# A diffusion trunk on one core: conditioning blocks taken later, stores delayed, a shorter lead of filling work in the output projection, and a final norm by products with ones

## The chip, the cores and the metric

The kernel runs on one core of one Trainium2 chip. The metric is the device time of one execution in microseconds (us), the median of several. Engines are named as the profile names them: PE (TensorE matmul) with PEld (its weight loads), DVE (VectorE), ACT (ScalarE), POOL (GpSimd), SP (SyncE, which here only issues DMAs). PEclk is the granted TensorE clock, 1.00 for 2.4 GHz and 0.50 for 1.2 GHz.

## The reference

A trunk of two layers over 1,152 positions (1,024 of a sample and 128 of a prompt), model width 1,024, everything in fp32. Layer 0 has an input projection that feeds attention heads and retention heads, layer 1 a gated MLP; each layer ends its first half with an output projection and its second half is a SwiGLU. Six vectors for each layer (shift, scale and gate, twice) come from the conditioning vector `c` by one product with `w_ada`.

```python
for l in range(DEPTH):
    sh1, sc1, g1, sh2, sc2, g2 = ada_mod(c, w_ada[l], b_ada[l])   # silu(c) @ w_ada + b_ada, 6 x 1024
    h = modulate(rmsnorm(x, norm_g[l, 0]), sh1, sc1)
    y = ab_latent(h, ...) if l % 2 == 0 else chunk_gmlp(h, ...)   # each ends in a product with w_o_ab / w_out_c
    x = x + g1 * y
    h = modulate(rmsnorm(x, norm_g[l, 1]), sh2, sc2)
    x = x + g2 * (silu(h @ w_ffn_gate) * (h @ w_ffn_up)) @ w_ffn_down
y = rmsnorm(x, final_norm_g)                                      # x / sqrt(mean(x*x) + eps) * g
```
The prompt runs through the same code with its own conditioning vector `c_ctx`.

## The kernel before

**Precision and tiling.** Every large product is made of three: an operand is split into a high part, which ACT rounds (CAST), and the low part that remains, which DVE subtracts (TENSOR_TENSOR). A weight tile is called `w0` to `w4` (a ring of five; two halves, high and low), its raw form lands in one of three slots of the tile `ST`. PE can start a weight's group when the high half is there, and goes on when the low half is. A group of products on PE is six matmuls of 288, 384 or 512 columns. Activations are feature-major, 128 features on the partitions; a piece `(c, h)` is 288 positions, c = 0, 1 and h = 0, 1. `x0` to `x3` hold the residual stream, `hq0` to `hq3` and `h0` to `h2` operands of products.

**Order.** The program is written by a planner. `Clocks` keeps a modelled time for each engine (`clk.t["T"]` is PE's); each instruction that is recorded moves it (so nearly all have the helper's line L129). `Stream.pump` goes through the list of weight loads: it issues the next load on SP as soon as one of the three slots is free, and when the load is ready by the model it writes the work on it. An entry of kind "w" is a weight (cast and difference). An entry of kind "pair" is a block of `w_ada`: two loads of 512 KB, and four matmuls in which `S32` (the conditioning vector, 32 columns) meets 512 columns of `ST`. SP issues in program order, so a load whose slot is not yet free keeps everything behind it waiting. `fill` writes work from three queues (squares, norms, splits of activations into high and low parts) as long as the modelled clocks of the other engines stay within `ahead[0]` of PE's (7.0 us; the SwiGLU sets its own). `tick`, after every group of products, calls both.

**Stages.** Up to 240 us: loads, norm, the attention heads' input projection; to 400 us: the other blocks of the input projection (with the second half of layer 0's conditioning), retention; to 735 us: attention; to 855 us: `proj_out` of layer 0; to 1655 us: SwiGLU by seven products of halves in the place of eight; to 1900 us: gated MLP (with layer 1's conditioning); to 2040 us: `proj_out` of layer 1; to 2818 us: the second SwiGLU; then the final norm and the stores.

**The output projection.** For each group of 288 columns, `resid` adds the gated product to `x` (DVE, SCALAR_TENSOR_TENSOR with `mod`), `squares` sums the squares over features for the next norm, and `pspill` stores the piece of `x` to DRAM (`xtd`, SP). When c = 0 is complete, `rscale` norms it and `rsplit` makes the 14 operands of the SwiGLU (sums, differences, high and low parts) as filling work, while PE goes on with c = 1. Four groups use one weight.

**The tail.** In the last projection, `last1` squares each finished piece: ACT makes the square in one of two buffers, multiplies x by the norm's gain, and DVE adds the square to the sum, one piece after the other. `done1` then norms c: `rstd` sums over the partitions by products with ones (96x2), root, reciprocal (both 96x12), a diagonal form, a second product that spreads the result over 128 partitions, and eight multiplications (128x576) whose results are stored on SP.

Of the kernel before, what the change touches and what calls it, by code (L numbers as in the profile page):

```python
# [13 lines left out]
P = 128  # L14
# [118 lines left out]
def body(nc, tc, ap):  # L133
# [88 lines left out]
    class Stream:  # L222
# [11 lines left out]
        def pump(self, force=False):  # L234
            moved = True
            while moved:
# [18 lines left out]
                if self.pi < self.di and self.pi not in self.stops:  # L255
# [4 lines left out]
                    if it["kind"] == "pair":  # L260
                        if self.pi + 1 >= self.di:
                            continue
                        two = self.items[self.pi + 1]
                        if not force and clk.ready([it["v"], two["v"]]) > clk.t["T"]:
                            continue
# [79 lines left out]
    def bg_add(gen):  # L345
        bg.append(gen)
        return gen
# [30 lines left out]

    def tick():
        W.pump()  # L380
        fill()
# [83 lines left out]
    def acc2(c):  # L465
        return SC[:, 1152 * c:1152 * c + 576]

    def piece(c, h):
        return 576 * h + HN * c
# [5 lines left out]
    def xp(f, c, h):  # L475
        return xh(c, f // 4)[:, f % 4, h]

    def xp2(i, c, h):
        return xh(c, i // 2)[:, 2 * (i % 2):2 * (i % 2) + 2, h]

    def pspill(i, c, h):
        o = piece(c, h)
        SY.dma_start(out=xtd[:, 2 * i:2 * i + 2, o:o + HN], in_=xp2(i, c, h))

# [76 lines left out]
    def xnorm(l, w, c):  # L561

        yield from rstd(c)
        A, B = acol[l][w], mod[l][:, 24 * w:24 * w + 8]
# [51 lines left out]
    def rscale(l, c, h):  # L616

        yield from rstd(c, (h,))
        A, B = acol[l][1], mod[l][:, 24:32]
# [1176 lines left out]
    def proj_out(l, bef=None, done=None, ks=range(8), mix=None):  # L1796
# [36 lines left out]
        drain(sq[0])  # L1833
        rplaces(0)
        for z in (FIRST_Q, OTHER_Q):
            bg_add(rsplit(0, z))
# [634 lines left out]


    def last1(c, m):
        for f in (m, m + 4):
            for h in range(2):
                x = xp(f, c, h)
                bg3.append(squares(c, h, f, lambda x=x, f=f: S.activation(x, x, AF.Copy, scale=P2[:, 19 + f:20 + f])))

    def done1(c):
        def gen():  # L2480
            yield from rstd(c)
            for h in range(2):
                r = acc2(c)[:, HN * h:HN * h + HN].unsqueeze(1).to_broadcast([P, 2, HN])
                for i in range(4):
                    x = xp2(i, c, h)
                    V.tensor_tensor(x, x, r, ALU.mult)
                    o = piece(c, h)
                    SY.dma_start(out=ap["o_y"][2 * i:2 * i + 2, :, o:o + HN].rearrange("f p t -> p f t"), in_=x)
                    yield
        g = bg_add(gen())  # L2490
        if c:
            drain(g)

# [58 lines left out]
```

## Time and profile before

| | before |
|---|---|
| median of 3 runs | 2847.53 us (2843.91 to 2848.49) |
| profiled execution | 2844.86 us |
| its span, first to last instruction | 2843.1 us |
| granted clock of PE, mean over the span | 0.983 |
| PE busy | 2689.3 us (95%) |
| DVE, ACT, POOL busy | 1787.7 us (63%), 1167.8 us (41%), 514.5 us (18%) |
| DMA moved | 457.67 MB, mean 161 GB/s |

The profile shows the span in 40 slices, then groups of instructions, the idle time of each engine with what ended it, and the chain of work that ended last. About 2 us of the execution's time lie outside its span. A row of a timeline is one run of like instructions on one engine: start, length, engine, operation, output<-inputs, shape, count, and in brackets the idle time ahead of it with what ended it.

### The profile page before, as it was taken

How to read it: one execution, taken by the hardware profiler on the slowest of the kernel's cores; microseconds unless marked ns; L12 is line 12 of the kernel's file. 1: busy time of each engine (PE TensorE's matmuls, PEld its weight loads, DVE VectorE, ACT ScalarE, POOL GpSimd, SP SyncE). 2: the span in 40 equal slices, each digit the busy share in tenths (PEclk: the TensorE clock that was granted, in tenths of full speed). 3: DMA queues.
4: the chain of work that ended last, by engine and by line, in shares of the span. 5: the costliest groups of instructions: out<-in, count | busy, mean ns of one | idle time of the engine just before them, and what ended most of it. 6: DMA issues, size and time to landing. Idle time of an engine off the chain costs nothing.

```text
span 2843.1 us, 49004 instructions
## 1 busy us (share of the span) xinstructions
PE 2689.3 (95%) x18859; PEld 2536.9 (89%) x18859; DVE 1787.7 (63%) x3606; ACT 1167.8 (41%) x2389; POOL 514.5 (18%) x570
## 2 busy tenths in 40 slices
PE   6989998999999999999999899998999999999996
PEld 5987897988988999999899877798999999999995
DVE  5651235888577565665788763456666666558876
ACT  5552224777455333333322351234544344332224
POOL 1120013665100000000465300000000000016551
PEclk9999998999999999999999999999999999999998
DMA  9386426323433444538877442352334343578761
GB/s 301 90 271 207 131 72 188 90 57 96 156 111 120 144 169 140 181 128 273 270 236 251 142 154 82 111 169 77 113 124 162 108 157 124 189 267 267 233 211 67
DMA packets 455328, 457.67 MB, mean 161 GB/s; under 512 B 25963, under 2 KB 399478, under 8 KB 453558
## 3 DMA queue, kind: packets, MB, share of 16 engines
q1 hardware_dynamic: 400272, 360.83, 41.3%
q10 hardware_dynamic: 54822, 93.70, 8.9%
q8 instruction: 149, 2.44, 0.4%
q14 instruction: 85, 0.70, 0.1%
HBM read 312.52 MB, written 141.93 MB: 160 GB/s over the span
## 4 chain that ended last, share of the span: by engine, by line
PE 62%; DVE 9%; ACT 4%; DMA 4%; issue 2%; POOL 1%; ACTq 0%; SPq 0%; DVEq 0%; POOLq 0%
PE PS L129 62%; DVE x L129 4%; DVE SC L129 2%; DVE w L129 2%; DMA hcd<-SC 2%; ACT x L129 1%; ACT w L129 1%; ACT SC L129 1%; DVE hq L129 1%; POOL ST L129 1%; DMA x<-xtd 0%; DMA w<-krd 0%; DMA ST<-in_w_ada 0%; DVE ST L129 0%; ACTq L129 0%
## 5 line engine op out<-in xcount | busy, mean ns | idle before, releaser
L129 PE MATMUL PS<-hq,w 128*128 128x288 f32 (+1 forms) x10644 | 1547.5, 302 | 62.6 <-ACT SC L129 16.2
L129 PEld LDWEIGHTS PS<-hq,w 128*128 128x128 f32 x10644 | 1484.3, 189 | 99.1 <-ACT w L129 20.8
L129 DVE TENSOR_TENSOR w<-ST,w 128x512 fp32r<-128x512 f32 (+3 forms) x539 | 382.1, 725 | 294.8 <-ACT w L129 290.4
L129 ACT CAST w<-ST 128x512 fp32r<-128x512 f32 (+3 forms) x717 | 375.2, 552 | 420.8 <-POOL ST L129 274.3
L129 DVE SCALAR_TENSOR_TENSOR x<-PS,mod,x 128x288 f32<-128x288 f32 (+2 forms) x944 | 389.5, 445 | 124.5 <-PE PS L129 119.4
L129 POOL TENSOR_TENSOR w<-ST,w 128x256 fp32r<-128x256 f32 (+1 forms) x178 | 126.9, 729 | 1592.2 <-ACT w L129 970.2
L129 PE MATMUL PS<-h,w 128*128 128x288 f32 (+1 forms) x2522 | 386.8, 298 | 10.7 <-DVE SC L129 7.3
L129 PEld LDWEIGHTS PS<-h,w 128*128 128x128 f32 (+1 forms) x2522 | 350.6, 188 | 21.5 <-DVE SC L129 9.7
L129 ACT COPY SC<-PS 128x576 f32<-128x576 f32 (+8 forms) x245 | 124.3, 510 | 259.8 <-PE PS L129 218.5
L129 PE MATMUL PS<-x,w 128*128 128x288 f32 (+1 forms) x1440 | 218.8, 299 | 1.8 <-ACT adac L129 1.4
L129 PEld LDWEIGHTS PS<-x,w 128*128 128x128 f32 x1440 | 203.0, 188 | 4.2 <-ACT h L129 1.8
L129 DVE TENSOR_TENSOR SC<-PS,SC 128x576 f32<-128x576 f32 (+3 forms) x146 | 94.1, 646 | 169.0 <-PE PS L129 149.0
L129 POOL TENSOR_TENSOR ST<-ST 128x256 f32<-128x256 f32 (+1 forms) x192 | 139.9, 729 | 150.6 <-DVE w L129 134.6
L129 PEld LDWEIGHTS PS<-w,hq 128*128 128x128 f32 x648 | 120.5, 188 | 38.9 <-issue 11.4
L129 PE MATMUL PS<-w,hq 128*128 128x512 f32 x648 | 154.6, 396 | 0.0
L129 DVE TENSOR_TENSOR SC<-SC 128x288 f32<-128x288 f32 (+5 forms) x215 | 104.4, 494 | 57.5 <-ACT SC L129 41.4
L129 ACT ACTIVATE SC<-SC 128x576 f32<-128x576 f32 (+2 forms) x89 | 56.9, 639 | 192.2 <-DVE SC L129 180.5
L129 PE MATMUL PS<-w,w 96*128 96x512 f32 x384 | 109.2, 420 | 4.7 <-ACT w L129 2.7
L129 DVE TENSOR_TENSOR SC<-SC,x 128x576 fp32r<-128x576 f32 (+1 forms) x90 | 68.0, 756 | 69.6 <-DMA hcd<-SC 50.7
L129 DVE TENSOR_REDUCE sm<-PS 128x1 f32<-128x1152 f32 (+1 forms) x72 | 89.0, 1236 | 21.9 <-PE PS L129 21.1
L129 ACT ACTIVATE SC<-x 128x288 f32<-128x288 f32 x128 | 55.2, 440 | 114.8 <-DVE x L129 92.4
L129 DVE TENSOR_TENSOR ST<-ST 128x512 f32<-128x512 f32 x144 | 98.8, 686 | 1.8
(191 smaller groups left out, 2475.9 us busy)
## 6 DMA issues: line engine op xcount, KB each, us to landing
hq<-hcd SPq DMA_DIRECT2D x106, 576.0 KB, 9.1
hcd<-x ACTq DMA_DIRECT2D x180, 288.0 KB, 2.2
ST<-in_w_ada SPq DMA_DIRECT2D x80, 512.0 KB, 4.2
h<-hcd SPq DMA_DIRECT2D x48, 576.0 KB, 7.3
ST<-in_w_ffn_gate SPq DMA_DIRECT2D x52, 512.0 KB, 4.0
ST<-in_w_ffn_up SPq DMA_DIRECT2D x52, 512.0 KB, 3.9
hcd<-SC ACTq DMA_DIRECT2D x72, 288.0 KB, 3.3
ST<-in_w_ffn_down SPq DMA_DIRECT2D x80, 256.0 KB, 5.4
```

The lines of the kernel that those rows point to most:

```text
L129: return fn(*args, **kw)
```

## The change

Four things change. A "pair" is written 1.5 us of modelled time later than before. `pspill` no longer stores at once: the stores stand in a list `due`, and `spill_due` issues them from `tick` 3.0 us after they are ready by the model, or at the latest where the norm begins to overwrite the same piece. In `proj_out`, the lead of filling work is 4.5 in the place of 7.0 from the point where c = 0 is complete. The tail is rewritten: of c = 1 only the first half of the squares is summed by DVE; the eight others go to buffers of their own, and ten products with ones (128x288) sum everything over the features and spread it in one step; root and reciprocal are 128x288, once for each h; four multiplications of c = 0 and their stores wait for the tail, and half of the last stores are issued by ACT.

```diff
                         two = self.items[self.pi + 1]
-                        if not force and clk.ready([it["v"], two["v"]]) > clk.t["T"]:
+                        if not force and clk.ready([it["v"], two["v"]]) + 1.5 > clk.t["T"]:
                             continue
...
     def tick():
+        spill_due()
         W.pump()
         fill()
...
+    due = deque()
+
     def pspill(i, c, h):
         o = piece(c, h)
-        SY.dma_start(out=xtd[:, 2 * i:2 * i + 2, o:o + HN], in_=xp2(i, c, h))
+        due.append((c, h, xtd[:, 2 * i:2 * i + 2, o:o + HN], xp2(i, c, h)))
+
+    def spill_due(which=None):
+
+        for z in list(due):
+            if z[:2] == which or which is None and clk.ready([z[3]]) + 3.0 < clk.t["T"]:
+                SY.dma_start(out=z[2], in_=z[3])
+                due.remove(z)
...
     def rscale(l, c, h):
 
+        spill_due((c, h))
         yield from rstd(c, (h,))
...
         rplaces(0)
+        ahead[0] = 4.5
         for z in (FIRST_Q, OTHER_Q):
             bg_add(rsplit(0, z))
...
     def last1(c, m):
+        if c and m > 1:
+            return
         for f in (m, m + 4):
...
     def done1(c):
         def gen():
-            yield from rstd(c)
+            yield from rstd(0)
             for h in range(2):
+                if h:
+                    yield lambda: False
+                yield from scaled_out(0, h, acc2(0)[:, HN * h:HN * h + HN])
+        if c == 0:
+            bg_add(gen())
+            return
+        while bg3:
+            bg_step(bg3)
...
+        late = [(0, 2), (0, 3), (1, 6), (1, 7), (1, 2), (1, 3), (0, 6), (0, 7)]
+
+        def add(h, q, st, sp):
+            TE.matmul(sums[h], lhsT=ones, rhs=q, start=st, stop=sp, skip_group_check=True)
+        for n, (h, f) in enumerate(late):
+            q = SC[:, 1728 + HN * n:][:, :HN] if n < 6 else adac[:, 0:HN] if n == 6 else ST[:, 0, 0:HN]
+            S.activation(q, xp(f, 1, h), AF.Square)
+            add(h, q, n in (0, 2), n in (5, 7))
+            if n == 3:
+                for z in range(2):
+                    add(z, a[:, HN * z:HN * z + HN], False, False)
+        for f in (2, 3, 6, 7):
+            gcol(1, 1, f)
+        for h in (1, 0):
+            S.activation(root[h], sums[h], AF.Sqrt, bias=epsc, scale=1.0 / 1024.0)
+        for f in (2, 3, 6, 7):
+            gcol(1, 0, f)
+        while bg:
+            bg_step()
+        for h in (1, 0):
+            V.reciprocal(root[h], root[h])
+            for _ in scaled_out(1, h, root[h]):
+                pass
```

`scaled_out` holds the four multiplications and stores that stood in `done1`; with c = 1 every other store goes to ACT's queue. `gcol` is the multiplication by the gain.

**Conditioning blocks on PE.** These are PE's rows at the start of the second part of the input projection, 241 us into the run. Rows with `ST_65,S32_92` are a pair; all others are groups of products. Before:

```order
L129 MATMUL PS_74<-hq3_20_535,w4_32_1715 128x384 x6
L129 MATMUL PS_74<-ST_65,S32_92 32x512 x4
L129 MATMUL PS_74<-hq0_13_219,w4_32_1715 128x384 x6
L129 MATMUL PS_74<-hq1_17_331,w4_32_1715 128x384 x6
L129 MATMUL PS_74<-hq2_19_465,w4_32_1715 128x384 x6
L129 MATMUL PS_74<-hq3_20_535,w4_32_1715 128x384 x6
L129 MATMUL PS_74<-ST_65,S32_92 32x512 x4
L129 MATMUL PS_74<-w0_33_1848,hq0_13_219 128x512 x6
L129 MATMUL PS_74<-w3_34_1852,hq1_17_331 128x512 x6
L129 MATMUL PS_74<-w1_35_1856,hq2_19_465 128x512 x6
L129 MATMUL PS_74<-ST_65,S32_92 32x512 x4
```

The same place of the change:

```order
L129 MATMUL PS_74<-hq0_13_219,w4_32_1715 128x384 x6
L129 MATMUL PS_74<-hq1_17_331,w4_32_1715 128x384 x6
L129 MATMUL PS_74<-hq2_19_465,w4_32_1715 128x384 x6
L129 MATMUL PS_74<-hq3_20_535,w4_32_1715 128x384 x6
L129 MATMUL PS_74<-ST_65,S32_92 32x512 x4
L129 MATMUL PS_74<-w0_33_1848,hq0_13_219 128x512 x6
L129 MATMUL PS_74<-w3_34_1852,hq1_17_331 128x512 x6
L129 MATMUL PS_74<-w1_35_1856,hq2_19_465 128x512 x6
L129 MATMUL PS_74<-w2_37_1970,hq3_20_535 128x512 x6
L129 MATMUL PS_74<-ST_65,S32_92 32x512 x4
```

The first pair has moved behind four groups of 384 columns, and the pairs that follow stand four groups of 512 columns apart, where three stood between them.

**Weights in the second output projection on DVE.** These are DVE's rows in `proj_out` of layer 1, 1979 to 1992 us into the run. The rows on `x0` and `x1`, `hq2`, `h0` and `h2` are the filling work of `rsplit`; `w2_142` and `w0_143` are the low halves of the next two weights. Before:

```order
L129 TENSOR_TENSOR x1_102_11573<-x1_102_11573,x0_101_11572 128x2x288 x2
L129 TENSOR_TENSOR hq2_19_465<-x1_102_11573,hq2_19_465 128x2x288 x2
L129 TENSOR_TENSOR h0_138_17472<-x0_101_11572,h0_138_17472 128x576 x2
L129 TENSOR_TENSOR x1_102_11573<-x1_102_11573 128x2x288 x2
L129 TENSOR_TENSOR h2_140_17474<-x1_102_11573,h2_140_17474 128x576 x2
L129 SCALAR_TENSOR_TENSOR x3_104_11716<-PS_74,mod1_94,x3_104_11716 128x288
L129 TENSOR_TENSOR w2_142_17618<-ST_65,w2_142_17618 128x1024
L129 TENSOR_TENSOR SC_66<-SC_66 128x288
L129 SCALAR_TENSOR_TENSOR x3_104_11716<-PS_74,mod1_94,x3_104_11716 128x288
L129 TENSOR_TENSOR w0_143_17650<-ST_65,w0_143_17650 128x1024
```

The same place of the change:

```order
L129 TENSOR_TENSOR x1_102_11573<-x1_102_11573,x0_101_11572 128x2x288 x2
L129 SCALAR_TENSOR_TENSOR x3_104_11716<-PS_74,mod1_94,x3_104_11716 128x288
L129 TENSOR_TENSOR w2_142_17604<-ST_65,w2_142_17604 128x1024
L129 TENSOR_TENSOR hq2_19_465<-x1_102_11573,hq2_19_465 128x2x288
L129 TENSOR_TENSOR SC_66<-SC_66 128x288
L129 TENSOR_TENSOR hq2_19_465<-x1_102_11573,hq2_19_465 128x2x288
L129 TENSOR_TENSOR h0_138_17471<-x0_101_11572,h0_138_17471 128x576 x2
L129 TENSOR_TENSOR x1_102_11573<-x1_102_11573 128x2x288 x2
L129 TENSOR_TENSOR h2_140_17473<-x1_102_11573,h2_140_17473 128x576 x2
L129 SCALAR_TENSOR_TENSOR x3_104_11716<-PS_74,mod1_94,x3_104_11716 128x288
```

The low half of `w2` has moved ahead of eight rows' worth of filling work (`hq2`, `h0`, `x1`, `h2`, two instructions each); that of `w0` stands behind all of it, as before. The low half of `w1`, a little earlier, has moved the other way, behind the norm's sixteen instructions, and `proj_out` of layer 0 shows the like: there the low halves of two weights move forward by some instructions each.

**The tail on DVE.** These are DVE's last rows before the change and in it. `x2` and `x3` are the pieces of c = 1, `x0` and `x1` of c = 0. Before:

```order
L129 SCALAR_TENSOR_TENSOR x3_159_22642<-PS_74,mod1_94,x3_159_22642 128x288 x2
L129 TENSOR_TENSOR SC_66<-SC_66 128x288 x13
L129 RECIPROCAL rs96_100<-rs96_100 96x12
L129 TENSOR_TENSOR SC_66<-ident_87,rs96_100 96x576
L129 TENSOR_TENSOR x2_158_22500<-x2_158_22500,SC_66 128x2x288 x2
L129 TENSOR_TENSOR x3_159_22642<-x3_159_22642,SC_66 128x2x288 x2
```

The same place of the change:

```order
L129 SCALAR_TENSOR_TENSOR x3_159_22642<-PS_74,mod1_94,x3_159_22642 128x288 x2
L129 TENSOR_TENSOR x0_156_22498<-x0_156_22498,SC_66 128x2x288 x2
L129 TENSOR_TENSOR x1_157_22499<-x1_157_22499,SC_66 128x2x288 x2
L129 RECIPROCAL SC_66<-SC_66 128x288
L129 TENSOR_TENSOR x2_158_22500<-x2_158_22500,SC_66 128x2x288 x2
L129 TENSOR_TENSOR x3_159_22642<-x3_159_22642,SC_66 128x2x288 x2
L129 RECIPROCAL SC_66<-SC_66 128x288
```

The thirteen additions behind the last product are gone (five of them stand among the earlier rows, eight are no longer there), two wide reciprocals have come, and each is followed by four multiplications (those after the second are the last four rows).

## Rows read from the trace of the kernel before

**Rows 1.** What PE waited for over the span: the engine and tile that ended the idle time, us in total, times, longest.

```profile
PE PS L129 <- DVE SC L129: 22.6, 13, 10.3
PE PS L129 <- ACT w L129: 22.1, 10, 9.5
PE PS L129 <- DVE w L129: 8.3, 7, 4.1
PE PS L129 <- DMA ST<-in_w_ada: 7.6, 4, 2.9
```

**Rows 2.** PE's timeline from 238 to 267 us (the conditioning blocks of layer 0; rows with ST,S are pairs, whose matmuls leave two records each).

```profile
241.25 2.87 PE L129 MATMUL PS<-ST,S 128*32 128x512 f32 x8 [2.88 <-DMA ST<-in_w_ada]
244.04 5.37 PE L129 MATMUL PS<-hq,w 128*128 128x384 f32 x24
...
254.67 1.05 PE L129 MATMUL PS<-ST,S 128*32 128x512 f32 x4
256.85 1.05 PE L129 MATMUL PS<-ST,S 128*32 128x512 f32 x4 [1.13 <-DMA ST<-in_w_ada]
257.83 4.41 PE L129 MATMUL PS<-w,hq 128*128 128x512 f32 x18
262.17 1.06 PE L129 MATMUL PS<-ST,S 128*32 128x512 f32 x8
```

**Rows 3.** One stretch of a table by windows (us, then the busy time of PE, PEld, DVE, ACT and POOL with counts, the granted clock, the DMA share, GB/s), and the row on loads of `w_ada` from the DMA view of 236 to 290 us (KB each, median us from issue to landing).

```profile
242.60:246.00 3.40, 3.40 (x10) 1.96 (x7) 0.00 (x0) 0.00 (x0) 0.00 (x0) 0.51 0.70 210
...
ST<-in_w_ada SPq DMA_DIRECT2D x16, 512.0 KB, 4.4
```

**Rows 4.** The output projection of layer 0: PE from 797 to 813 us, then DVE in the same stretch.

```profile
803.49 5.65 PE L129 MATMUL PS<-hq,w 128*128 128x288 f32 x22 [4.08 <-DVE w L129]
810.81 2.37 PE L129 MATMUL PS<-hq,w 128*128 128x288 f32 x16 [0.73 <-DVE w L129]
...
797.78 1.42 DVE L129 TENSOR_TENSOR x<-x,x 128x576 f32<-128x576 f32 x2
802.22 1.21 DVE L129 TENSOR_TENSOR w<-ST,w 128x1024 fp32r<-128x1024 f32 x1
806.42 1.42 DVE L129 TENSOR_TENSOR x<-x 128x576 f32<-128x576 f32 x2
```

**Rows 5.** The output projection of layer 1: PE from 1964 to 1998 us, then DVE, then one window (columns as in rows 3).

```profile
1989.33 0.85 PE L129 MATMUL PS<-hq,w 128*128 128x288 f32 x2 [9.47 <-ACT w L129]
1990.73 7.51 PE L129 MATMUL PS<-hq,w 128*128 128x288 f32 x45 [0.56 <-DVE w L129]
...
1983.52 1.43 DVE L129 TENSOR_TENSOR hq<-x,hq 128x576 fp32r<-128x576 f32 x2
1989.46 1.21 DVE L129 TENSOR_TENSOR w<-ST,w 128x1024 fp32r<-128x1024 f32 x1
1991.39 1.21 DVE L129 TENSOR_TENSOR w<-ST,w 128x1024 fp32r<-128x1024 f32 x1
...
1989.30:1993.50 4.20, 3.62 (x13) 3.27 (x14) 4.20 (x8) 2.76 (x5) 0.00 (x0) 0.50 0.35 89
```

**Rows 6.** The conditioning blocks of layer 1, 1836 to 1870 us: PE, then SP's issues.

```profile
1841.70 1.06 PE L129 MATMUL PS<-ST,S 128*32 128x512 f32 x8
...
1856.85 1.75 PE L129 MATMUL PS<-ST,S 128*32 128x512 f32 x8
...
1842.80 0.81 SPq L129 DMA_DIRECT2D ST<-in_w_ada  x2
1848.81 0.38 SPq L129 DMA_DIRECT2D ST<-in_w_in_c  x1
```

**Rows 7.** The tail, 2806 to 2844 us: PE's last four rows, then DVE, ACT and SP.

```profile
2816.88 0.96 PE L129 MATMUL PS<-h,hq 128*128 128x288 f32 x6
2828.10 2.08 PE L129 MATMUL PS<-ones,SC 128*96 128x2 f32 x12 [10.26 <-DVE SC L129]
2831.66 2.29 PE L129 MATMUL PS<-SC,ones 96*128 96x288 f32 x4 [1.47 <-DVE SC L129]
...
2817.68 0.93 DVE L129 SCALAR_TENSOR_TENSOR x<-PS,mod,x 128x288 f32<-128x288 f32 x2
2833.45 5.44 DVE L129 TENSOR_TENSOR x<-x,SC 128x576 f32<-128x576 f32 x8 [1.85 <-ACT SC L129]
...
2819.01 0.44 ACT L129 ACTIVATE SC<-x 128x288 f32<-128x288 f32 x1 [1.97 <-DVE SC L129]
2819.49 0.53 ACT L129 ACTIVATE x<-x,P 128x288 f32<-128x288 f32 x1
...
2834.24 5.09 SPq L129 DMA_DIRECT2D o_y<-x  x8
```

**Rows 8.** DVE's reciprocals, grouped by form over the whole span (output<-input with the shape, count, busy us in all, mean ns of one).

```profile
L129 DVE RECIPROCAL sm<-sm 128x1 f32<-128x1 f32 x72 | 10.5, 156 | 11.4 <-ACT SC L129 11.3
L129 DVE RECIPROCAL rcn<-rcn 128x18 f32<-128x18 f32 x4 | 1.1, 266 | 9.0 <-ACT rcn L129 9.0
```

**Rows 9.** PE, 2801 to 2806 us: one product with ones (96x288, two records) between products at the full clock.

```profile
2802.08 0.65 PE L129 MATMUL PS<-SC,ones 96*128 96x288 f32 x2
2802.35 1.18 PE L129 MATMUL PS<-h,w 128*128 128x288 f32 x6
2803.37 0.65 PE L129 MATMUL PS<-SC,ones 96*128 96x288 f32 x2
```

More of the change, by code (lines that the diff above doesn't have):

```diff
@@ L561, in xnorm @@
     def xnorm(l, w, c):
+        for h in range(2):
+            spill_due((c, h))
         yield from rstd(c)
@@ L616, in rscale @@
     def rscale(l, c, h):
+        spill_due((c, h))
         yield from rstd(c, (h,))
@@ L2470, in body, with gcol, scaled_out @@
     yield "E"
+    def gcol(c, h, f):
+        x = xp(f, c, h)
+        S.activation(x, x, AF.Copy, scale=P2[:, 19 + f:20 + f])
     def last1(c, m):
+        if c and m > 1:
+            return
         for f in (m, m + 4):
             for h in range(2):
-                x = xp(f, c, h)
-                bg3.append(squares(c, h, f, lambda x=x, f=f: S.activation(x, x, AF.Copy, scale=P2[:, 19 + f:20 + f])))
+                bg3.append(squares(c, h, f, lambda h=h, f=f: gcol(c, h, f)))
+    def scaled_out(c, h, r):
+        for i in range(4):
+            x = xp2(i, c, h)
+            V.tensor_tensor(x, x, r.unsqueeze(1).to_broadcast([P, 2, HN]), ALU.mult)
+            o = piece(c, h)
+            (SY if i % 2 or not c else S).dma_start(out=ap["o_y"][2 * i:2 * i + 2, :, o:o + HN].rearrange("f p t -> p f t"), in_=x)
+            yield
@@ L2479, in done1 @@
     def done1(c):
         def gen():
-            yield from rstd(c)
+            yield from rstd(0)
             for h in range(2):
[L2483 to L2489, printed above, removed]
@@ L2490, in done1 @@
-        g = bg_add(gen())
-        if c:
-            drain(g)
+                if h:
[6 more added lines that the diff above has]
+            bg_step(bg3)
+        a = acc2(1)
+        sums = [PS[:, 4 + h, :HN] for h in range(2)]
+        root = [SC[:, 576 + HN * h:][:, :HN] for h in range(2)]
+        late = [(0, 2), (0, 3), (1, 6), (1, 7), (1, 2), (1, 3), (0, 6), (0, 7)]
```

## Prediction

> **What bounds the kernel now.** I read first what PE waits for [rows 1], since PE is busy for 95% of the span: only its idle time and its time at the half clock can be won. Four waits stand out: on sums of squares from DVE, on the high and the low halves of weights, and on conditioning loads. Then I followed each one in the timelines. The conditioning loads stop PE at the start of the second part of the input projection [rows 2]; the halves of weights stop it in both output projections [rows 4, 5]; the sums stop it in the tail [rows 7]. After each of the longer stops the granted clock is 0.50 for some us [rows 3, 5], so a stop costs more than its length.
>
> **The conditioning blocks of layer 0.** PE waits 2.88 us for the first pair, which then takes 2.87 instead of 1.06 us because its second load lands late; of the groups behind it, 3.4 us run at 0.51 of the clock [rows 2, 3]. Four groups of 512 columns would follow at 1.45 us each (257.83 to 262.17 for three), so four of 384 are worth 4 x 1.45 x 384/512 = 4.3 us; they took 5.3 (244.04 to 249.34). The pair at 254.67 ends 3.16 us later, for its second load lands late again. What can be removed: 2.88 + 1.81 + 1.0 + 2.1 = 7.8 us. In the change the first pair stands four groups later, at 241.25 - 2.88 + 4.3 = 242.7; its data were there at 241.25 and, for the second load, some 2 us after. The later pairs stand 4 x 1.45 + 1.0 = 6.8 us apart in the place of 5.3. A pair's loads can start when the one before gives its slots back, and take 0.8 to issue and 4.4 to land [rows 3]: 5.2 us, which just fits into 5.3 and has 1.6 to spare in 6.8. I take -7.5; bounds -8.2 (the casts behind gain a little too) and -4 (the first pair still waits for its second load and brings the half clock with it). What is moved behind them, casts and norm factors, is used tens of us later and hides behind products.
>
> **Layer 1's conditioning blocks** move by a group or more. One of them takes 1.75 in the place of 1.06 us [rows 6], so there is 0.7 to win, twice or three times that if others gain as much, and nothing at worst: -0.7.
>
> **The delayed stores.** On SP they stand in the change behind one or two loads of weights rather than ahead of them. A load can't start before its slot is free, and in the projections that is when the low half of an earlier weight is made; an issue of 0.4 us, like those of weights [rows 6], ahead of it is hidden by that wait. I cost it at nothing; with the cover gone it is eight stores of 0.4 us, 3 us either way. The norm that overwrites a piece now waits for a store that may have been issued late; queued behind it on DVE are the operands of the SwiGLU and the low halves of weights, and PE waits for those. It is the third rival below that would show it.
>
> **The shorter lead, layer 0.** PE stops 4.08 us for the low half of `w1` at 802.22 [rows 4]. In the change it stands ahead of the work at 797.78 and is ready before PE asks at 799.4. The stop then falls on the next weight, `w0`: four groups later PE asks for it at 802.6. DVE has the same work ahead of it as before, but for the work at 806.42 and behind, which it now overtakes: 806.4 + 0.4 + 1.2 = 808.1, where PE went on at 810.81 before. That is 2.5 us earlier; but the stop is now one of 5.5 us and the half clock falls on products that before ran at the full one (22 matmuls took 5.65 us at 803.49, 16 took 2.37 at 810.81). I take -0.5; bounds -2.5 and +1.
>
> **The shorter lead, layer 1.** PE stops 9.47 us for the high half of `w2` and 0.56 for its low half, made at 1989.46 [rows 5]. In the change the low half stands in front of the work that began at 1983.52. The half of `w1` that moved the other way makes DVE about 1 us later there: 1983.5 + 1.0 + 0.4 + 1.2 = 1986.1. PE starts 4 us earlier, at the half clock; four groups of 1.6 us (13 matmuls took 3.62) bring it to 1992.5. The low half of the next weight, `w0`, was made at 1991.39, ending 1992.6; with DVE 1 us late it ends at 1993.5, and PE came to it at about 1995 before (24 matmuls from 1989.33, the first 13 of them at the half clock). So 4 us earlier become 1.5: the stop is split in two. I take -1.5; bounds -2.6 and 0.
>
> **The tail.** The last product begins at 2816.88 and DVE's last piece of x ends at 2818.6 [rows 7]. Before, eight squares and additions run in turn, ACT 0.44 + 0.53 us each, up to 2828.1; then products with ones at the half clock, root, reciprocal, diagonal, a second product, copy, and at 2833.45 eight multiplications of 0.68 us. The last store is issued at 2839.3 and the span ends at 2843.1.
>
> In the change PE follows its last product without a stop: a product with ones costs 2802.08 to 2803.37 less the six matmuls between (0.80), 0.49 us [rows 9]. Eight of the ten make the sum of h = 1: 2817.7 + 8 x 0.49 = 2821.6. ACT's last square ends at about 2819.1 and its four multiplications by the gain at 2821.2, so PE decides. The root, 0.4 us like ACT's other operations on 288 columns, gives 2822.0. DVE has by then done c = 0's four multiplications (2818.6 + 2.7 = 2821.3).
>
> The trace has no reciprocal of 288 columns. From 1 to 18 columns it grows from 156 to 266 ns [rows 8], 6.5 ns a column: 0.15 + 287 x 0.0065 = 2.0 us. The bound below is the square of 288 columns on ACT, 0.44 [rows 7]; the one above is proportion to the widest row, 266/18 x 288 = 4.3 us. I take 2.0, since the slope is of the operation itself. The Trainium skill ("VectorE: DVE Perf Modes", First, the fixed hardware budget, and its table of specifications) says that the reciprocal is an iterative divide that repeats 8 times, at 0.96 GHz. An estimate by that page is 8 x 288 cycles, 2.4 us, plus the fixed part, 2.55 in all, and the tail 1.1 us worse than in my sum; the trace's 6.5 ns a column against 8.3 speaks for less.
>
> So: reciprocal to 2824.0, four multiplications to 2826.8, reciprocal to 2828.8, four to 2831.5. Each store is 288 KB; the eight of before took 5.09 us to issue and the DMA kept up. The span ended 3.8 us after the last issue; I keep that: 2835.4 for 2843.1, -7.6 when rounded. Bounds: a reciprocal of 0.44 would give 3 us more, but with 288 KB behind each multiplication the stores' transfer then decides, and I give it 2, -9.5; the products with ones at the half clock, like those at 2831.66 (1.15 us each), cost 8 x 0.65 = 5, and leave -3.
>
> **The sum.** -7.5 - 0.7 + 0 - 0.5 - 1.5 - 7.6 = -17.8 us. Against the profiled execution, 2844.86, that is 2827.1. It was 2.7 below the median of the runs shown (2847.53), whose own sum is 2829.7; I say 2828.5.
>
> **The rivals.**
> First, the conditioning wait moves rather than goes: the second load of the first pair is still late, the half clock comes back. For it: 16 loads of 512 KB stand one behind the other, and the loads of weights between them. Against: 1.6 us to spare in each interval. The term is then -3 and the time 2833.
>
> Second, the tail eats its gain: PE idles between products with ones, since each waits for its square, and runs at 0.50; or the reciprocals take near 4.3 us, 2 x 2.3 more. For it: nothing here shows ones at 288 columns in a row. The term is -3, the time 2833. With the first rival as well it is 2838.
>
> Third, the splits of the two output projections each bring a stop with a half clock of its own behind it: +3 each, in the place of -2, and 2836.
>
> Fourth, the one that ends slower: starved weights in the gated MLP. SP issues in order, and the next weight's load stands behind the loads of a conditioning pair, which wait for the pair before to be multiplied. Before, those at 1842.80 were free 1.1 us after the pair at 1841.70, and the weight's load followed at 1848.81 [rows 6]. In the change that pair stands about 4.3 us later, near 1846: loads at 1846.2, issued by 1847.0, 1.8 us before the weight's own slot is free. If PE's place were over 1.8 us later than the planner's, the weight would be late, and so each of eight weights, by up to the 4.3 us of a group of four: +34 at most, +16 with the rest of the sum, 2861.
>
> That the change does not do what it says can be for the stores alone, and is in the sum already.
>
> **How the numbers follow.** The forecast 0.55, the first rival 0.15, the second 0.14, the third 0.06, both of the first two 0.05, the fourth 0.05. The likeliest case spreads by the bounds that oppose each other: some 6 us to either side. The range 2819 to 2839 holds the forecast and the first three rivals and leaves out the fourth, the edges of the combination and a gain of more than -28. About 0.2%, 5.7 us, is what a measurement of this kernel can tell from no change. All cases but the fourth end below 2841.8, with the combination near it: faster 0.88, same 0.07, slower 0.05.
>
> **What the profile would show.** Right: no idle ahead of the pairs from 240 to 290 us and a clock of 1.00 there; ten products with ones at 0.49 us; reciprocals of 2.0 us; the first of the last eight multiplications at 2824 less what was won before; PE's stop in layer 1's projection of about 6 us, with a second one of 1 us. Wrong: waits on `in_w_ada` with a clock of 0.50 in rows like [rows 3]; waits on DMA for `in_w_in_c` from 1690 to 1880 us, which would be the fourth rival; reciprocals beyond 2.7 us; the stores' transfer ending more than 5 us after the last multiplication.

## The result

| | before | changed |
|---|---|---|
| median (6 runs each, same chip) | 2848.01 us (2843.91 to 2853.06) | 2830.76 us (2827.8 to 2840.64) |
| profiled execution, span | 2844.86, 2843.1 us | 2827.8, 2825.6 us |
| ratio, 95% interval | | 0.9949, 0.9935 to 0.9964 |

The change makes the kernel faster by 0.0051 x 2848 = 14.5 us (10 to 18.5). The two profiled executions differ by 17.5 us in span; the forecast sum was 17.8. That nearness is partly luck, as the experiments show: one term was more than twice too large for the kernel as it mostly runs, one was put down to the wrong edit, and a stretch at the full clock that the forecast doesn't hold filled the hole.

What PE waits for in the changed kernel, over the whole span (us in total, times, longest), against [rows 1]:

```profile
PE PS L129 <- ACT w L129: 16.9, 9, 4.2
PE PS L129 <- DVE SC L129: 10.4, 10, 1.6
PE PS L129 <- DVE w L129: 9.3, 7, 4.4
PE PS L129 <- DMA ST<-in_w_ada: 3.5, 3, 2.6
```

The wait on DVE's sums has lost the 10.3 us of the tail and some more, the one on high halves has lost its 9.5 us and gained 4.0 in layer 0, the one on conditioning loads has halved, and the one on low halves has grown by a microsecond.

**The conditioning blocks**, to be read against [rows 2]. PE in the changed kernel from 236 to 254 us:

```profile
235.71 9.87 PE L129 MATMUL PS<-hq,w 128*128 128x384 f32 x56
245.51 1.07 PE L129 MATMUL PS<-ST,S 128*32 128x512 f32 x8
246.51 5.78 PE L129 MATMUL PS<-w,hq 128*128 128x512 f32 x24
252.22 1.15 PE L129 MATMUL PS<-ST,S 128*32 128x512 f32 x8
```

No idle time stands ahead of a pair, each takes 1.1 us, and they are 6.7 us apart (6.8 was forecast).

**The output projections.** PE in layer 0, against [rows 4], and then PE and DVE in layer 1, against [rows 5]:

```profile
802.84 0.53 PE L129 MATMUL PS<-hq,w 128*128 128x288 f32 x2 [4.00 <-ACT w L129]
804.44 10.73 PE L129 MATMUL PS<-hq,w 128*128 128x288 f32 x60 [1.07 <-DVE w L129]
...
1979.64 5.26 PE L129 MATMUL PS<-hq,w 128*128 128x288 f32 x22 [4.38 <-DVE w L129]
1985.70 0.54 PE L129 MATMUL PS<-hq,w 128*128 128x288 f32 x2 [0.80 <-ACT w L129]
1987.11 3.24 PE L129 MATMUL PS<-hq,w 128*128 128x288 f32 x14 [0.88 <-DVE w L129]
...
1967.73 1.22 DVE L129 TENSOR_TENSOR w<-ST,w 128x1024 fp32r<-128x1024 f32 x1 [1.49 <-ACT w L129]
1978.37 1.21 DVE L129 TENSOR_TENSOR w<-ST,w 128x1024 fp32r<-128x1024 f32 x1
1985.84 1.22 DVE L129 TENSOR_TENSOR w<-ST,w 128x1024 fp32r<-128x1024 f32 x1
```

In layer 0 the stop has moved to the next weight and is 5.1 us in all for 5.2. In layer 1 the 10.0 us have become 4.4, then 0.8 and 0.9.

**The tail**, against [rows 7] and [rows 8]. PE, DVE and ACT, then the wide reciprocal in the view by forms:

```profile
2807.89 4.04 PE L129 MATMUL PS<-SC,ones 128*128 128x288 f32 x16
2811.76 0.65 PE L129 MATMUL PS<-adac,ones 128*128 128x288 f32 x2
...
2812.50 1.95 DVE L129 RECIPROCAL SC<-SC 128x288 f32<-128x288 f32 x1 [1.23 <-ACT SC L129]
2814.49 2.77 DVE L129 TENSOR_TENSOR x<-x,SC 128x576 f32<-128x576 f32 x4
2817.17 1.95 DVE L129 RECIPROCAL SC<-SC 128x288 f32<-128x288 f32 x1
2819.15 2.77 DVE L129 TENSOR_TENSOR x<-x,SC 128x576 f32<-128x576 f32 x4
...
2811.96 0.50 ACT L129 ACTIVATE SC<-PS,epsc 128x288 f32<-128x288 f32 x1 [1.18 <-PE PS L129]
...
L129 DVE RECIPROCAL SC<-SC 128x288 f32<-128x288 f32 x2 | 3.9, 1950 | 1.2 <-ACT SC L129 1.2
```

PE goes from its last product (2807.09) to the ones without a stop. Eight of them end 3.87 us later, 0.48 each. From the start of the first product with ones to the end of the span it is 17.7 us. (From the last product's own start it is 18.5 us, for 26.2 in the kernel before; the 17.7 and 25.4 of the expectations below are counted from where the next product can begin, 0.8 us later.) The chain that ends last here is DVE's: reciprocal, four multiplications, reciprocal, four multiplications, without a gap between the second and the third of these.

### The profile page after: what moved, and what is told of

Its sections match the earlier page's. It is cut to its first block, busy times and chain, and to the rows that moved or that the text cites. A ratio compares the mean times of both kernels' runs of the same rounds, so it can differ in the third digit from the quotient of the medians.

```text
span 2825.6 us, 48991 instructions
## 1 busy us (share of the span) xinstructions
PE 2692.8 (95%) x18863; PEld 2544.6 (90%) x18863; DVE 1787.4 (63%) x3598; ACT 1168.3 (41%) x2388; POOL 514.5 (18%) x570
## 4 chain that ended last, share of the span: by engine, by line
PE 64%; DVE 9%; ACT 3%; DMA 3%; issue 2%; POOL 1%; ACTq 0%; SPq 0%; DVEq 0%; POOLq 0%
PE PS L129 64%; DVE x L129 4%; DVE SC L129 2%; DVE w L129 2%; DMA hcd<-SC 2%; ACT x L129 1%; ACT w L129 1%; ACT SC L129 1%; DVE hq L129 1%; POOL ST L129 0%; DMA w<-krd 0%; DMA ST<-in_w_ada 0%; DMA ST<-in_w_in_c 0%; DVE ST L129 0%; ACTq L129 0%
```

## The experiments

Times wander: the kernel before had medians from 2848 to 2854.5 us in the different sets of runs, and its single executions on one chip lay up to 21 us apart. So besides the ratio I compare stretches. All kernels issue the same products in the same order on PE (only the pairs, the products with ones and a few small products beside the pairs move), so the start of the same product can be looked up in two traces. The table gives the length of a stretch between two products, minus its length in the first profile of the kernel before (us, worked out from one profiled execution of each kernel; columns are named by the time in that first profile; the tail runs from 2816 us to the end). The second column is a part of the first: it begins at a product just ahead of the pairs that move, and so leaves out what differs before them.

| kernel | 200-400 | 233-400 | 400-735 | 735-830 | 830-1665 | 1665-1880 | 1955-2022 | 2022-2816 | tail |
|---|---|---|---|---|---|---|---|---|---|
| whole change | -6.9 | -7.9 | +1.0 | -0.35 | -1.7 | +0.6 | -1.3 | -3.2 | -7.69 |
| whole change, again | -5.8 | -7.8 | +4.3 | -0.34 | +5.1 | +1.4 | -1.5 | +0.2 | -7.67 |
| before, again | -5.7 | -7.4 | +2.4 | +0.63 | +5.9 | +4.8 | +0.1 | +3.4 | +0.01 |
| pairs alone | -5.2 | -7.3 | +3.7 | +0.02 | +3.1 | +1.1 | +1.2 | -1.8 | +0.28 |
| stores alone | -4.4 | -4.4 | +1.5 | +0.05 | +2.8 | +3.0 | -2.8 | +6.0 | +0.01 |
| lead alone | -3.9 | -4.0 | +3.9 | -0.33 | +0.5 | +0.9 | +2.9 | +2.6 | -0.07 |
| tail alone | -4.0 | -3.6 | +2.7 | +0.01 | +1.0 | +0.0 | +0.0 | +1.8 | -7.67 |
| without the lead | -7.4 | -7.7 | +3.9 | +0.05 | +2.9 | -0.3 | -3.0 | +2.1 | -7.68 |
| without the pairs | -3.9 | -5.7 | +3.4 | -0.34 | +2.1 | +2.1 | -1.3 | -1.1 | -7.68 |
| pairs later still | -6.0 | -7.4 | +5.0 | -0.35 | -0.3 | +11.7 | -1.3 | +0.8 | -7.68 |
| one queue | -6.0 | -7.7 | +1.5 | -0.37 | +0.0 | -0.3 | -1.5 | +1.3 | -7.69 |
| h = 1 first | -7.0 | -7.3 | +2.8 | -0.35 | +4.6 | +0.8 | -3.0 | -1.9 | -8.96 |
| h = 1 first, POOL | -7.8 | -7.6 | +5.0 | -0.37 | +5.1 | -1.9 | -2.9 | +2.6 | -7.42 |

Three columns repeat to a few tenths: the two projections (735-830, 1955-2022) and the tail. One row of them stands out: with the pairs alone, 1955-2022 is +1.2, with the same stops of 9.47 and 0.56 us as before; the 64 matmuls behind them took 11.27 us for 10.04. In 233-400 the later pairs repeat (-7.3 to -7.9), the old order doesn't. In the others executions of like order differ by several us (400-735 and 830-1665, which hold nearly nothing of the change, spread over 4 and 7.6 us).

### The parts alone

Later pairs alone:

```diff
-if not force and clk.ready([it["v"], two["v"]]) > clk.t["T"]:
+if not force and clk.ready([it["v"], two["v"]]) + 1.5 > clk.t["T"]:
```

> The kernel before with the later conditioning pairs alone (+ 1.5 in the planner's test), nothing else. My theory: PE has no idle time and no half clock between 240 and 290 us, and the products behind 400 us start 7.5 us earlier against those ahead of 235 us than in the kernel before; the gated MLP adds 0 to -0.7; span -7.5 to -8. Rival (the wait only moves): an idle time ahead of a later pair, a stretch at 0.50, and -3. Rival (weights of the gated MLP starve): idle time on in_w_in_c after 1690 us and a span that is longer.

Measured: 0.9973 (0.9958 to 0.9987), which is 7.7 us (3.7 to 12). PE has no idle time between 240 and 290 us and the clock is 1.00; one pair, at 253.12, takes 1.72 us for 1.06. From the product at 233 us to 400 us the execution is 7.3 us shorter than the first profile, as expected (7.5). In the stretch 200-400 it is 5.2, since 2.2 us were lost ahead of the pairs. What this is worth stands or falls with what the unchanged order takes, below.

Delayed stores alone:

```diff
 def pspill(i, c, h):
     o = piece(c, h)
-    SY.dma_start(out=xtd[:, 2 * i:2 * i + 2, o:o + HN], in_=xp2(i, c, h))
+    due.append((c, h, xtd[:, 2 * i:2 * i + 2, o:o + HN], xp2(i, c, h)))
```

(with `spill_due` and its calls)

> The kernel before with the delayed stores alone. In my prediction they were worth nothing. The order of its program says something else: in the second output projection the low half of w2 has moved forward on DVE here already, as in the whole change, and that of w1 backward, behind the norm and the first operands; in the first one nothing of the kind. If the stores move the planner's clocks and so the weights, PE's stop of 9.47 us in layer 1 splits: about 1.5 to 3 us for w1 near 1977, then some 4 us for w2; the span is -3 to +1. If the stores are without effect on the time (my prediction), the stop stays near 9.5 us and the span at 0.

Measured: 0.9988 (0.9972 to 1.0003). The time tells nothing, the trace does. PE in layer 1's projection, and the norm's first work on DVE:

```profile
1966.72 0.67 PE L129 MATMUL PS<-ones,SC 128*96 128x2 f32 x6
1987.82 4.72 PE L129 MATMUL PS<-hq,w 128*128 128x288 f32 x22 [2.89 <-DVE w L129]
1993.89 0.53 PE L129 MATMUL PS<-hq,w 128*128 128x288 f32 x2 [1.35 <-ACT w L129]
1995.30 7.05 PE L129 MATMUL PS<-hq,w 128*128 128x288 f32 x40 [0.88 <-DVE w L129]
...
1970.03 3.52 DVE L129 SCALAR_TENSOR_TENSOR x<-x,acol,SC 128x288 f32<-128x288 f32 x8 [1.14 <-ACT SC L129]
1979.18 1.22 DVE L129 TENSOR_TENSOR w<-ST,w 128x1024 fp32r<-128x1024 f32 x1
```

The stop of 10 us is 5.1 us here, with no change of the lead. The stop that I expected for `w1` near 1977 did not come. The norm's eight multiplications on DVE begin 3.3 us behind the norm's products with ones (1966.72), and the low half of `w1` stands behind them. In the kernel before, the low half and a piece of `x3` came first, and they began 5.1 us behind (1963.82 and 1968.95):

```profile
1963.82 0.39 PE L129 MATMUL PS<-ones,SC 128*96 128x2 f32 x3
...
1967.22 0.52 DVE L129 SCALAR_TENSOR_TENSOR x<-PS,mod,x 128x288 f32<-128x288 f32 x1 [1.93 <-PE PS L129]
1967.81 1.23 DVE L129 TENSOR_TENSOR w<-ST,w 128x1024 fp32r<-128x1024 f32 x1
1968.95 0.51 DVE L129 SCALAR_TENSOR_TENSOR x<-x,acol,SC 128x288 f32<-128x288 f32 x1
```

So the stores' gain is not in the stores. Taking them out of the modelled order lets the planner write the norm earlier, ahead of an eviction that waits 1.93 us for PE; and the low half of `w2` (1986.56) stands here ahead of the last eight rows of filling work, as in the whole change. By the low half of `w0` the same work is done as before, 1.7 us earlier (1994.03, in an execution that is 4.4 us behind the first profile at 1955 us, for 1991.39). (Why the planner's clocks do so was read from the code only: a store that reads `x` holds back, by the model, what overwrites it.)

The shorter lead alone:

```diff
         rplaces(0)
+        ahead[0] = 4.5
```

> The kernel before with the lead of 4.5 in proj_out alone. My prediction gave the lead -0.5 in layer 0 and -1.5 in layer 1. The order of this program has, in layer 1, the low halves of both w2 and w0 moved forward (to before the work at 1975 and at 1983.5), which the whole change has not. If both count, PE does not stop for w2 at all, and stops about 3 us for w0 near 1983, without or with a short half clock: -5 to -8 in layer 1, -0.5 in layer 0. If the lead acts as in the whole change: one stop of 4.4 and one of 1.7 us, and -2 in all.

Measured: 1.0015 (1.0003 to 1.0028), slower if anything, and neither theory. PE from 1983 to 2003 us:

```profile
1983.81 0.54 PE L129 MATMUL PS<-hq,w 128*128 128x288 f32 x2 [0.32 <-ACT w L129]
1989.07 7.54 PE L129 MATMUL PS<-hq,w 128*128 128x288 f32 x40 [4.72 <-DVE w L129]
2001.27 1.12 PE L129 MATMUL PS<-ones,SC 128*96 128x2 f32 x6 [4.66 <-DVE SC L129]
2002.25 4.67 PE L129 MATMUL PS<-hq,w 128*128 128x288 f32 x18
```

`w2` is ready in time, as expected. But PE stops 4.72 us for `w0`, and then 4.66 us for the sum of squares that the next norm needs: DVE is late with its work whichever piece is put first, and 9.7 us of stops are merely cut in two. PE's half speed follows the last of them as well (18 matmuls in 4.67 us, at a clock of 0.50).

The tail alone:

```diff
+        for n, (h, f) in enumerate(late):
+            q = SC[:, 1728 + HN * n:][:, :HN] if n < 6 else adac[:, 0:HN] if n == 6 else ST[:, 0, 0:HN]
+            S.activation(q, xp(f, 1, h), AF.Square)
+            add(h, q, n in (0, 2), n in (5, 7))
...
+        for h in (1, 0):
+            V.reciprocal(root[h], root[h])
```

(and all else that the change does there)

> The kernel before with the new tail alone. My theory: from the last product's start to the end of the span 17.7 us for 25.4 before, -7.6, whatever stands ahead. Ones at 0.49 us each at the full clock, two reciprocals of 1.95 us. Rival (the gain needs what was won before, by the clock of PE): ones at about 1 us and 4 us less gain.

Measured: 0.9982 (0.9968 to 0.9996), and the tail is -7.67 us in the trace. In all kernels that have the new tail as it stands it is between -7.67 and -7.69.

### What the unchanged order takes in the conditioning blocks

The runs with the stores, the lead and the tail alone have the pairs where they stood, yet their stretch 200-400 is 4 us shorter than in the profile that I predicted from. So the kernel before was profiled once more.

> The kernel before, unchanged, profiled once more. In the runs with the stores, the lead or the tail alone, whose conditioning pairs stand as before, PE stopped for the first pair 0.5 to 1.1 us and not 2.88, and no stretch at the half clock followed; so the first profile would have caught an unlucky execution. If so, this one has a stop of 0.5 to 1.2 us at the first pair and the groups behind it at the full clock (24 matmuls of 384 columns in 4.4 us and not 5.4). If the unchanged kernel always stops for long, it shows 2.9 and 5.4 again.

PE in this second profile of the kernel before:

```profile
242.92 1.06 PE L129 MATMUL PS<-ST,S 128*32 128x512 f32 x8
243.92 4.46 PE L129 MATMUL PS<-hq,w 128*128 128x384 f32 x24
...
253.72 1.36 PE L129 MATMUL PS<-ST,S 128*32 128x512 f32 x8
```

and the first pair in the run with the stores alone:

```profile
240.37 2.20 PE L129 MATMUL PS<-ST,S 128*32 128x512 f32 x8 [0.61 <-DMA ST<-in_w_ada]
242.50 4.46 PE L129 MATMUL PS<-hq,w 128*128 128x384 f32 x24
```

Of six executions with the old order (the run without the pairs, below, is one), the stop is absent in two, 0.5 to 1.1 us in three and 2.88 in the first profile, the only one in which the 24 matmuls behind it took 5.37 us and not 4.46. What sets the stop is how far SP issues the pair's first load ahead of PE. These are the loads in the first profile and in the second; PE came to the pair at 238.37 and at 242.92 us:

```profile
237.12 0.82 SPq L129 DMA_DIRECT2D ST<-in_w_ada  x2
...
237.66 1.30 SPq L129 DMA_DIRECT2D ST<-in_w_ada  x3
```

In the four executions that stop, PE can go on 4.0 to 4.2 us after this issue. SP was 1.25 us ahead of PE in the first profile, 3.1 to 3.4 in the three short stops, 5.3 and 6.0 in the two without one. To be late as a whole is not enough: in the run with the lead alone PE came 0.5 us earlier than in the first profile and yet stopped for 0.54 us only.

The same question from the other side, the whole change with the pairs at their old place:

```diff
-if not force and clk.ready([it["v"], two["v"]]) + 1.5 > clk.t["T"]:
+if not force and clk.ready([it["v"], two["v"]]) > clk.t["T"]:
```

> The whole change with the pairs at their old place (stores, lead and tail stay). My prediction gave the pairs -8.2 (-7.5 and -0.7), so this would be 8 us slower than the whole change, -6 against the kernel before. By the stretches of the other runs (from 200 to 400 us the executions with later pairs won 6.3 us on the mean against the first profile, those without 3.6; from 1665 to 1880 another 1.0) the pairs are worth 2.7 + 1.0, so this would be some -10 to -11 against the kernel before, and its own stretch from 200 to 400 us shows -3 to -6.

Measured: 0.9951 (0.9931 to 0.997); the stretch 200-400 is -3.9. The time can't tell this from the whole change. The stretches can: with later pairs (seven executions at + 1.5) 200-400 is -6.6 on the mean, without (six) -3.7; 1665-1880 is +0.2 with and +1.8 without, in a wide scatter. Without what differs ahead of the pairs, from 233 to 400 us, it is -7.6 on the mean with later pairs, every execution between -7.3 and -7.9, and -4.2 without, between 0 and -7.4. So the later pairs take the wait out in every execution, and what that is worth depends on the execution of the unchanged order: 3.4 us on the mean in layer 0. In layer 1 it is perhaps 1.6, but the two groups overlap.

### Without the lead

```diff
         rplaces(0)
-        ahead[0] = 4.5
```

> The change without its lead of 4.5 (pairs, stores and tail stay). If the lead is worth what my prediction gave it (-2.0), this is 2 us slower than the whole change. The lead alone measured no gain, so my theory now is that it is worth nothing: in layer 0 the same 5 us of stops, in layer 1 stops of 5 to 6 us in all for DVE's backlog with or without it; the time within 2 us of the whole change on either side.

> The whole change once more, as the measure for the run without the lead and the one with pairs later still. By the sum of the runs of its parts, -7.7 for the pairs, -3.4 for the stores, -5.1 for the tail and +4.3 for the lead, it would be -12 against the kernel before; by its first measurement (0.9949) -14.5.

Measured on one chip: 0.9953 (0.9937 to 0.997) without the lead, 0.9947 (0.993 to 0.9965) with it. In layer 0 the lead wins 0.4 us (eight executions with it at -0.33 to -0.37; the six without, the first profile among them, from 0 to +0.63). In layer 1 it costs 1.6: -3.0 without, -1.3 to -1.5 with it, always beside the delayed stores. The ratios of the four parts alone add up to -12 us for -15.1 here, but each of them is uncertain by some 4 us to either side: the times don't test whether the parts add.

### Pairs later still

```diff
-if not force and clk.ready([it["v"], two["v"]]) + 1.5 > clk.t["T"]:
+if not force and clk.ready([it["v"], two["v"]]) + 4.5 > clk.t["T"]:
```

> The whole change with 4.5 in the place of 1.5 in the test for pairs. My theory: in the input projection nothing more can be won, since with 1.5 PE does not wait there any more, while SP's queue holds weights behind the loads of a pair: idle time on weights (in_w_in_ab after 290 us, in_w_in_c from 1690 us on) and a longer span by 3 to 20 us. Rival (every pair that comes later helps): shorter than the whole change.

Measured: 1.0 (0.9983 to 1.0017): all of the gain is gone, 15 us. In the profile 11 of them stand in 1665-1880; the rest is within what executions differ by. PE from 1689 us on, and its waits from 1660 to 1900 us:

```profile
1689.24 0.79 PE L129 MATMUL PS<-w,hq 128*128 128x512 f32 x1 [5.46 <-ACT w L129]
1691.69 5.01 PE L129 MATMUL PS<-w,hq 128*128 128x512 f32 x11 [1.66 <-DVE w L129]
...
PE PS L129 <- ACT w L129: 10.6, 6, 5.5
PE PS L129 <- DVE w L129: 6.1, 7, 1.7
```

PE waits for the halves of weights, 16.7 us in this stretch for 5.2 in the changed kernel's profile. Only a part of this is the fourth rival of the prediction, made to happen. The longest stops, 5.46 and 1.66, are not SP's: the load of this weight was issued at 1673.10, the DMA engines moved nothing from 1678 to 1684 us, and its cast on ACT came at 1688.16, behind ACT's work on operands and without a wait for a load:

```profile
1688.16 1.03 ACT L129 CAST w<-ST 128x1024 fp32r<-128x1024 f32 x1
```

`pump` goes through its list in order, so a weight that stands behind a pair is not written before the pair is (read from the code only). For PE's stops at 1840, 1871 and 1877 us the casts did wait for `in_w_in_c`, 1.83, 1.70 and 0.49 us, as the rival has it; these stops are 6.4 us, for 4.0 at two such places in the changed kernel. Behind these stands SP's queue, which issues a pair's loads only when the pair before has been multiplied, with the weights' loads behind them. What SP waited for PE from 1660 to 1900 us, in the kernel before, in the changed kernel and here:

```profile
SPq L129 <- PE PS L129: 41.4, 18, 6.6
```

```profile
SPq L129 <- PE PS L129: 46.6, 16, 8.4
```

```profile
SPq L129 <- PE PS L129: 79.1, 18, 10.2
```

With 1.5 the queue waits 5 us longer than before and PE feels nothing of it; with 4.5 it waits 38 us longer. Of the 11 us that PE loses, some 7 are the order in which the weight's halves are written, and some 2 the late loads.

### The tail: queues, order, POOL

All of the last stores on SP:

```diff
-(SY if i % 2 or not c else S).dma_start(out=ap["o_y"][2 * i:2 * i + 2, :, o:o + HN].rearrange("f p t -> p f t"), in_=x)
+SY.dma_start(out=ap["o_y"][2 * i:2 * i + 2, :, o:o + HN].rearrange("f p t -> p f t"), in_=x)
```

> The whole change with all of the last stores issued by SP. A store's issue took 0.64 us and its multiplication 0.69, so one queue keeps up and the tail from the last product's start to the end of the span stays at 17.7 us. Rival (two queues are part of the tail's gain): 1 to 3 us longer.

Measured: 0.9937 (0.9918 to 0.9957), tail -7.69. The second queue is worth nothing here.

The sum of h = 1 first, and the lead in layer 0 alone:

```diff
-            add(h, q, n in (0, 2), n in (5, 7))
-            if n == 3:
-                for z in range(2):
-                    add(z, a[:, HN * z:HN * z + HN], False, False)
+            made.append(q)
+        for h, ns in ((1, (2, 3, 4, 5)), (0, (0, 1, 6, 7))):
+            add(h, a[:, HN * h:HN * h + HN], True, False)
+            for n in ns:
+                add(h, made[n], False, n == ns[-1])
...
-        ahead[0] = 4.5
+        if l == 0:
+            ahead[0] = 4.5
```

> The whole change with the lead of 4.5 in layer 0 alone, and in the tail the five products with ones of h = 1 ahead of the five of h = 0. The sum of h = 1 is then there 3 products of 0.49 us earlier; the root starts behind ACT's four gains at 2810.8 and not at 2812.0, so the two reciprocals and the eight multiplications, which decide the end, start 1.2 us earlier: tail 16.5 for 17.7. In layer 1's projection the stop is that of the change without the lead: 1.4 us less on the mean of the runs. Together -2 to -3 against the whole change. Rival (the transfer of the stores decides, not DVE): the tail stays at 17.7.

Measured: 0.9926 (0.9914 to 0.9939), 2833.03 us where the kernel before had 2854.53: 21 us, the lowest ratio of all, though its interval overlaps those of the runs beside it. DVE in the tail:

```profile
2817.54 1.95 DVE L129 RECIPROCAL SC<-SC 128x288 f32<-128x288 f32 x1
2819.53 2.76 DVE L129 TENSOR_TENSOR x<-x,SC 128x576 f32<-128x576 f32 x4
```

The reciprocal no longer waits for ACT; the tail is 1.27 us shorter and the projection 1.5, as expected of each.

One multiplication of each h on POOL:

```diff
-            V.tensor_tensor(x, x, r.unsqueeze(1).to_broadcast([P, 2, HN]), ALU.mult)
+            (G if c and i == 3 else V).tensor_tensor(x, x, r.unsqueeze(1).to_broadcast([P, 2, HN]), ALU.mult)
```

> As the run before it, with one of the four multiplications of each h on GpSimd. POOL's rows for 128x256 take 0.73 us, so 128x576 is some 1.65; it runs beside DVE's second reciprocal. If DVE's chain decides, it loses 2 x 0.69 = 1.4 us, and the last store comes from whichever ends later: 0.7 to 1.4 us less. If DVE and POOL hinder each other, or the transfer decides: no gain, or a loss up to 1 us.

Measured: 0.9938 (0.9926 to 0.9951), the tail 1.54 us longer than in the run before it, more than either theory had. DVE and POOL, and the second of the three multiplications on DVE by itself:

```profile
2822.93 3.31 DVE L129 TENSOR_TENSOR x<-x,SC 128x576 f32<-128x576 f32 x3
2822.98 1.98 POOL L129 TENSOR_TENSOR x<-x,SC 128x576 f32<-128x576 f32 x1 [39.15 <-DVE SC L129]
...
2823.61 1.96 DVE L129 TENSOR_TENSOR x<-x,SC 128x576 f32<-128x576 f32 x1
```

Three multiplications on DVE take 3.31 us beside POOL's; four take 2.76 alone. Only the second is stretched: the first and the third take 0.76 and 0.74 us, the second begins while POOL's runs and ends 0.6 us behind it. So the three cost more than the four. Whether POOL is hindered too isn't shown, since no run has its multiplication without DVE's beside it.

## Why the prediction was right, and where it was not

**The conditioning blocks of layer 0: -7.5 forecast, -3.4 on the mean.** The mechanism was right, no idle time and 6.7 us between the pairs. So was the size against the profile that it was read from: all seven executions with later pairs are 7.3 to 7.9 us shorter than that one from 233 to 400 us. It was not the size for the kernel. The step that failed is "What can be removed: 2.88 + 1.81 + 1.0 + 2.1 = 7.8 us": it took the execution with the longest stop of six for the kernel before, whose second profile lost nothing there (-7.4). Even the bound of -4 was beyond the mean. The working itself gave a hint: loads of 5.2 us that "just fit" into 5.3 make a wait that depends on when PE arrives, so one execution's wait is no size. The time of the pairs alone, 7.7 us (3.7 to 12), can't tell the forecast from the mean.

**Layer 1's blocks: -0.7 forecast;** -1.6 on the mean of 7 and 6 executions that lie between -1.9 and +4.8. The two groups overlap, so not even the sign is settled.

**The stores: nothing forecast; -3.0 in layer 1's projection.** The step that failed is that I costed the moved SP issues and not what their leaving does to the planner. I gave the moves on DVE in that projection to the lead, because they show in the whole change; the order of the kernel with one part alone tells whose they are.

**The lead.** Layer 0: -0.5 forecast, -0.4. Its working holds as well: PE goes on at 804.44 in an execution that is 3.85 us ahead of the first profile at 735 us, so at 808.3 for the 808.1 forecast. Layer 1: -1.5 forecast for it, and that stretch is -1.3 to -1.5; yet it is the sum of -3.0 from the stores and +1.6 from the lead. By the third rival each stop would be split in two and be dearer; the lead alone did that in layer 1, at +2.9 against the rival's +3, and not in layer 0.

**The tail: -7.6 forecast, -7.68.** Its terms hold too: ones at 0.48 us for 0.49, reciprocals at 1.95 for 2.0, multiplications 0.69 for 0.68, the end 3.7 us behind the last of them. The slope of 1 to 18 columns carried to 288. The estimate by the Trainium skill ("VectorE: DVE Perf Modes", First, the fixed hardware budget), 2.55 us, was too long by 0.6; the measured (1950 - 156)/287 is 6.3 ns a column.

**The sum.** By the means of the stretches: -3.4 - 1.6 - 0.4 - 1.4 - 7.7 = -14.5, and the two measurements of the whole change are -14.5 and -15.1 (0.0053 x 2852.8). Such a match is better than the terms are known. The forecast's -17.8 met the 17.5 of the two profiles because the first of them had the long stop and the second was 3.2 us shorter from 2022 to 2816. The first rival's number (-3 for that term) came nearer to the mean than the forecast, but not its mechanism: from 240 to 290 us the changed kernel has no idle time on PE and a clock of 1.00. Of the fourth rival a part becomes real with 4.5 in the test; where between 1.5 and 4.5 it sets in was not measured.

## What to carry to other kernels

A wait whose two sides wander against each other from one execution to the next (here a load's issue and PE, by 1.25 to 6.0 us) has no size in one profile: look at a second execution before it enters a sum, or take the bound. Where a planner sets the order, build each part alone and compare the orders ahead of any run; an edit that moves only DMA issues can move the compute of another engine. When an engine is behind with its whole work, putting another piece of it first moves the stop (10.0 us became 9.7 with the lead alone); to let the work begin earlier shortens it.

## What the runs showed of the hardware

Whether a short stop is followed by the half clock can differ between executions of the same order. Every execution has a stop of 1.8 us near 2025 us, for `x` from DVE. The last two runs of the tail have the same order up to there, and in the projection ahead of it PE stops 5.3 and 5.2 us in all; behind this stop PE ran at 2.4 GHz in the first and at 1.2 in the second (windows; us, PE busy, clock, DMA share, GB/s; the same products):

```profile
2026.30:2032.80 6.50, 6.50 (x52) 1.00 0.54 155
```

```profile
2025.30:2031.80 6.50, 6.50 (x30) 0.50 0.44 123
```

The half clock costs 3.1 us here. It followed in both profiles of the kernel before and in five others, and not in the two of the whole change and in five others. So the changed kernel's profile has 3 us over the first of the kernel before; whether they are chance or come from the later pairs (six of the eight profiles with them have the full clock, one of the six without) these runs don't show. In the second profile of the whole change the stretch 2022-2816 is +0.2 all the same: as much was lost further on.

And one elementwise engine can hold up another: a multiplication of 128x576 on DVE that began beside one of POOL took 1.96 us for 0.75. The Trainium skill ("SBUF — State Buffer", SBUF: two separate sides) says that a DVE operation with two SBUF inputs and a GpSimd operation that reads SBUF share a pair of ports, which the one that starts first holds for its whole instruction while the other waits. The trace agrees for DVE: its second multiplication ends 0.6 us behind POOL's, about the time that it takes alone, and its third is not stretched.
